# Two mixtures of experts with split fp32 weights: a slab's products ordered by weight part, and the second mixture's buffers cut six raw to four split

## The chip, the cores and the metric

The kernel runs on one core of a Trainium2 chip. The metric is the device time of one execution in microseconds: 3967.31 us is the median of three executions before the change (3966.20 to 3977.65). The trace comes from one more execution, which took 3961.94 us.

## The reference

Two transformer-like blocks follow each other on 1024 tokens of width 1024. Each ends in a mixture of experts, and only these two mixtures are touched. In the first, a router picks two of 32 experts for each token; in the second, each of 16 experts picks its 128 best tokens. What an expert does is the same in both:

```python
# first mixture, per expert e (D=1024, F=512)
hb = jax.nn.silu(xb @ w1[e]) * (xb @ w3[e]);  yb = hb @ w2[e]
# second mixture, all 16 experts (D=1024, F=2048)
gt = jnp.einsum('becd,edf->becf', xe, w_gate);  up = jnp.einsum('becd,edf->becf', xe, w_up)
ye = jnp.einsum('becf,efd->becd', jax.nn.silu(gt) * up, w_down) * vals[..., None]
x = x + jnp.zeros_like(x).at[bidx, idx].add(ye)
```

All data are fp32, and the result has to be near that of fp32.

## The kernel before

TensorE gets near fp32 by splitting. `split` (lines 41 to 44) makes of an fp32 tile a high part on ScalarE (`hi`, line 43, rounded to the matmul's own type) and the rest on VectorE (`lo`, line 44: source minus `hi`). `mm3` (lines 49 to 52) then sums three products into PSUM: high by high (L50), token-high by weight-low (L51), token-low by weight-high (L52). In the trace a matmul `h<-hi,xh` is L50, `h<-lo,xh` L51, `h<-hi,xl` L52. The tokens are the stationary operand, the weights the moving one of 512 columns, so each product loads the tokens anew (LDWEIGHTS, on the row PEld).

Weights come in slabs of 1 MB (`Unit.slab`): a raw tile of 128 partitions by 2048 numbers is asked for by a DMA on SyncE's queue, then split. Three rings of buffers pass a slab on: `raw` (pool `wraw`), and `hi` and `lo` (pool `whl`). A raw buffer is free again when `lo` is made; `hi` and `lo` are free when the slab's twelve products are done.

`Unit.up` makes silu(x W1)*(x W3) for 512 hidden columns: four slabs of four 128-row pieces each, twelve products a slab, into two PSUM tiles `h`. Then `u` is made on ScalarE and VectorE, transposed on TensorE (`pt<-ident,u`), and split into `hh` and `hl`. `Unit.down` multiplies them with two slabs into `y`, again twelve products a slab. `run_units` goes over the units; `up` of the next one stands before `down` of this one. The first mixture has 32 units of 96 tokens (one an expert; in 11 of them `down` uses raw fp32 weights, `rawn`, with no split), and beside it a filter's transform is made in small steps (`ks`, `kv`, `K_d`), called at each slab's end by `tick`. The second has 16 experts of four units each, 384 slabs in all, and nothing beside it.

A token list is looked up an expert ahead (`fetch` in `moe2`): one-hot rows `oh` on VectorE, eight small matmuls, the tile `pc` of one column, and a gather of rows `xg` by GpSimd. At an expert's end its rows `ys` are added to DRAM by a scatter on GpSimd's queue. Each engine works its instructions off in a fixed order; a scheduler has set that order when the program was built, from the order in which the code is written and the buffers that exist.

Of the kernel before, what the change touches and what calls it, by code (L numbers as in the profile page):

```python
# [11 lines left out]
F32=mybir.dt.float32; F32R=mybir.dt.float32r; I32=mybir.dt.int32; U32=mybir.dt.uint32  # L12
# [36 lines left out]
def mm3(nc, ps, sh, sl, mh, ml, start, stop):  # L49
    nc.tensor.matmul(ps, sh, mh, start=start, stop=False)  # L50
    nc.tensor.matmul(ps, sh, ml, start=False, stop=False)  # L51
    nc.tensor.matmul(ps, sl, mh, start=False, stop=stop)  # L52

def colmajor(ap, n):

    return ap.rearrange("(n p) -> p n", p=128)
# [23 lines left out]
def flat(ap):  # L80
    return ap.rearrange("p a b -> p (a b)")

def bcast_row(ap, n, off=0):

    return bass.AP(tensor=ap.tensor,offset=ap.offset+off,ap=[[0,128],[1,n]])
# [371 lines left out]
SPL=1  # L457
# [170 lines left out]
class Unit:  # L628
# [26 lines left out]
    def up(s,x,w1,w3,nat=False):  # L655

        k,nc,p,m=s.k,s.k.nc,s.p,s.m
        xh,xl=x
        hs=[]
        for w in (w1,w3):  # L660
            ps=s.ph.tile([128,512],F32,name="h")[0:m]
            for c in range(2):
                sl=s.slab(w[512*c:512*c+512],4,512)
                for j in range(4):
                    d=4*c+j
                    mm3(nc,ps,xh[:,d],xl[:,d],*sl[j],d==0,d==7)
                s.tick()
            hs.append(ps)
        u=p.tile([128,512],F32,name="u")[0:m]
        nc.scalar.activation(u,hs[0],AF.Silu)  # L670
        nc.vector.tensor_tensor(u,u,hs[1],op=ALU.mult)
        ps=s.pt.tile([128,4,m],F32,name="pt")
        for j in range(4): nc.tensor.transpose(ps[:,j],u[:,128*j:128*j+128],k.ident[0:m,0:m])
        if nat:
            ht=p.tile([128,4,m],F32R,name="hh").bitcast(F32); nc.scalar.activation(ht,ps,AF.Copy)
            return ht,None
        hh=p.tile([128,4,m],F32R,name="hh"); hl=p.tile([128,4,m],F32R,name="hl")
        split(nc,hh,hl,ps)
        return hh,hl
    def down(s,h,w2,y,first,last):  # L680
        nc=s.k.nc
        hh,hl=h
        for c in range(2):
            src=w2[256*c:256*c+256]
            if hl is None:
                raw=s.wnat.tile([128,2048],F32,name="rawn")
                raw=raw.rearrange("p (k n) -> p k n",k=2); nc.sync.dma_start(raw,src.rearrange("(k p) n -> p k n",p=128))
                for j in range(2):
                    f=2*c+j
                    for n in range(2): nc.tensor.matmul(y[0:s.m,n],hh[:,f],raw[:,j,512*n:512*n+512],start=first and f==0,stop=last and f==3)  # L690
                s.tick()
                continue
            sl=s.slab(src,2,1024)
            for j in range(2):
                f=2*c+j
                for n in range(2):
                    st,sp=first and f==0,last and f==3
                    mm3(nc,y[0:s.m,n],hh[:,f],hl[:,f],*[q[:,512*n:512*n+512] for q in sl[j]],st,sp)
            s.tick()

def run_units(U,units,ahead):
# [21 lines left out]
        z=p.tile([128,256],F32,name="z"); nc.gpsimd.memset(z,0.0)  # L723
        for d in dst: nc.gpsimd.dma_start(d[1024:1152].rearrange("p (a b) -> p a b",b=256),z[:,None,:].to_broadcast([128,4,256]))

def moe_pools(tc,es,nb,pre,nr=4):

    e=lambda *x,**y: es.enter_context(tc.tile_pool(*x,**y))
    return e(name=pre+"r",bufs=nr if nb>1 else 2),e(name=pre+"w",bufs=3*SPL if nb>1 else 2*SPL),e(name=pre,bufs=nb)

def moe1(k,a,R,fill):

# [803 lines left out]
def moe2(k,a,R,out):  # L1536
    tc,nc=k.tc,k.nc
    wg,wu,wd=a['w_gate_2'][0],a['w_up_2'][0],a['w_down_2'][0]
    acc_d,xn_d=R.acc_d,R.xn_d
    with ExitStack() as es:  # L1540
        pre=ExitStack(); pp=pre.enter_context(tc.tile_pool(name="m2p",bufs=1,side="right"))
        k.gathers=[]
        first=[pp.tile([128,2048],F32,name=f"pre{j}") for j in range(NPRE)]
        wraw,whl,p=moe_pools(tc,es,2,"m2",8)
        R.route()
        e=lambda *x,**y: es.enter_context(tc.tile_pool(*x,**y))
        ph,pt,py=e(name="m2h",bufs=4,space=PSUM),e(name="m2t",bufs=2,space=PSUM),e(name="m2y",bufs=1,space=PSUM)
# [2 lines left out]
        def unit(x,u):  # L1550
            c=slice(512*u,512*u+512)
            def fetch():
                sel=pt.tile([128,5],F32,name="pt")
                for t in range(8):
                    if t%4==0:
                        oh=p.tile([128,4,128],BF16,name="oh")
                        nc.vector.tensor_tensor(oh,R.iota[:,None,:].to_broadcast([128,4,128]),R.posT[:,t:t+4,x:x+1].to_broadcast([128,4,128]),op=ALU.is_equal)
                    nc.tensor.matmul(sel,oh[:,t%4],R.aux[:,t,x],start=t==0,stop=t==7)
                pc=p.tile([128,1],F32,name="pc"); nc.vector.tensor_copy(pc,sel[:,0:1])
                nc.vector.scalar_tensor_tensor(R.tok[:,x:x+1],sel[:,1:2],128.0,pc,op0=ALU.mult,op1=ALU.add)  # L1560
                nc.vector.tensor_reduce(R.aff[:,x:x+1],sel[:,2:5],axis=AX.X,op=ALU.add)
                return U.fetch(xn_d,R.tok[:,x:x+1])
            def down(h):
                if x==0 and u==0:
                    pre.close()
                    F['p']=e(name="fin",bufs=1,side="right"); F['w']=e(name="finw",bufs=6,side="right")
                if x==1 and u==0: F['gf']=F['p'].tile([128,1024],F32,name="gf"); nc.gpsimd.dma_start(F['gf'],bcast_row(a['g_final_2'],1024))
                if u==0: ys_[x]=py.tile([128,2,512],F32,name="y")
                U.down(h,wd[x][c],ys_[x],u==0,u==3)
            def fin():  # L1570
                y=ys_.pop(x)
                if x<15:
                    ys=p.tile([128,1024],F32,name="ys"); nc.scalar.activation(ys,flat(y),AF.Copy,scale=R.aff[:,x:x+1])
                    nc.gpsimd.indirect_dma_start(out=acc_d,out_offset=bass.IndirectOffsetOnAxis(ap=R.tok[:,x:x+1],axis=0),in_=ys,in_offset=None,compute_op=ALU.add)
                    if x==14: U.tick=lambda: next(last,None)
                else:
                    for _ in last: pass
                    z=F['rows']
                    nc.vector.scalar_tensor_tensor(z,flat(y),R.aff[:,x:x+1],z,op0=ALU.mult,op1=ALU.add)
                    r=unit_rows(k,F['p'],F['p'],z,"rd")  # L1580
                    nc.vector.scalar_tensor_tensor(z,z,r,F['gf'],op0=ALU.mult,op1=ALU.mult)
                    nc.gpsimd.indirect_dma_start(out=out,out_offset=bass.IndirectOffsetOnAxis(ap=R.tok[:,x:x+1],axis=0),in_=z,in_offset=None)
            return dict(fetch=fetch if u==0 else None,up=lambda q: U.up(q,wg[x][:,c],wu[x][:,c]),down=down,fin=fin if u==3 else None)

        F={}
# [19 lines left out]
        last=finish()  # L1605
# [52 lines left out]
```

## Time and profile before

| | us |
|---|---|
| median of three executions | 3967.31 |
| the profiled execution | 3961.94 |
| its span, first to last instruction | 3960.2 |
| first mixture, from its first weight product to the last of its `up` | 704 to 1466 |
| second mixture, from its token lists to its last products | 2776 to 3930 |

TensorE is busy 94% of the span, VectorE 78%, ScalarE 56%. Matmuls overlap each other in the trace (each is some 0.40 us long, and the next begins about 0.23 us after it), so the busy share does not tell how densely they follow; the starts do. The page's 40 slices, 99 us each, show TensorE near full in both mixtures (slices 7 to 14 and 28 to 39), and the DMA engines too. A row of waits reads: who waited, for whom, how long in all, how often, the longest.

### The profile page before, as it was taken

To read this page: it belongs to the slowest core of one execution; us is meant where nothing else is said; L and a number is where in the kernel's file an instruction comes from. 1 tells how busy PE (TensorE), PEld (TensorE's weight loads), DVE (VectorE), ACT (ScalarE), POOL (GpSimd) and SP (SyncE) were. 2 spreads that over 40 slices of the span, in tenths; PEclk is the share of its full clock that TensorE was granted. 3 is DMA by queue.
4 is the path that set the end of the run, shared out by engine and by line. 5 is a ranking of instruction groups with operands and counts; after the bars stand their busy time and mean duration, and the time that the engine had idled before them with its cause. 6 is when DMAs were issued, how large, how long until landed. Compare 5 with 4: busy or idle time off the path is not lost.

```text
span 3960.2 us, 49738 instructions
## 1 busy us (share of the span) xinstructions
PE 3733.2 (94%) x18392; PEld 2960.8 (75%) x18392; DVE 3080.9 (78%) x4728; ACT 2215.0 (56%) x2522; POOL 443.7 (11%) x469
## 2 busy tenths in 40 slices
PE   8999998899989996999999999997899999999997
PEld 6787676676766675777888887876677777777775
DVE  3655765899889886776899989644788888888887
ACT  3733653566656654884333333322577777777776
POOL 0013000323332221000000000000000100100100
PEclk9999898899999997999999999998899999999998
DMA  3235634899989974122333335635799999999997
GB/s 96 64 96 114 169 104 175 281 341 320 314 292 327 312 262 147 57 88 86 96 109 110 105 103 171 208 129 198 262 366 374 359 367 371 358 375 364 363 374 290
DMA packets 459240, 900.99 MB, mean 228 GB/s; under 512 B 41734, under 2 KB 140257, under 8 KB 458610
## 3 DMA queue, kind: packets, MB, share of 16 engines
q1 hardware_dynamic: 414578, 801.90, 58.2%
q0 software_dynamic: 42832, 92.21, 8.4%
q10 hardware_dynamic: 1584, 3.67, 0.3%
q8 instruction: 146, 2.39, 0.3%
q14 instruction: 100, 0.82, 0.1%
HBM read 795.27 MB, written 102.29 MB: 227 GB/s over the span
## 4 chain that ended last, share of the span: by engine, by line
PE 60%; DVE 9%; issue 5%; DMA 5%; ACT 4%; POOL 1%; DVEq 0%; SPq 0%; ACTq 0%; POOLq 0%
PE h L51 7%; PE h L52 7%; PE h L50 7%; PE ps L51 5%; PE ps L52 5%; PE ps L50 5%; PE y L51 4%; PE y L52 4%; PE y L50 4%; PE iv L1086 3%; DVE lo L44 2%; DMA raw<-in_expert_w 2%; PE U L1074 1%; PE ks L1023 1%; PE y L690 1%
## 5 line engine op out<-in xcount | busy, mean ns | idle before, releaser
L44 DVE TENSOR_TENSOR lo<-raw,hi 128x2048 fp32r<-128x2048 f32 x551 | 1251.7, 2288 | 146.9 <-ACT hi L43 146.2
L43 ACT ACTIVATE hi<-raw 128x2048 fp32r<-128x2048 f32 x551 | 1047.9, 1913 | 222.7 <-PE h L52 114.2
L51 PE MATMUL h<-lo,xh 128*128 128x512 f32 (+1 forms) x1536 | 617.6, 402 | 12.5 <-DVE lo L44 12.5
L50 PE MATMUL h<-hi,xh 128*128 128x512 f32 (+1 forms) x1536 | 616.7, 402 | 0.6 <-ACT xh L43 0.6
L52 PE MATMUL h<-hi,xl 128*128 128x512 f32 (+1 forms) x1536 | 610.0, 397 | 0.0
L50 PE MATMUL ps<-hTh,whi 128*128 128x512 f32 x896 | 359.1, 401 | 2.8 <-ACT ge L1252 2.8
L51 PEld LDWEIGHTS h<-lo,xh 128*128 128x128 f32 (+1 forms) x1536 | 276.9, 180 | 105.2 <-DVE lo L44 33.2
L51 PE MATMUL ps<-hTl,whi 128*128 128x512 f32 x896 | 354.9, 396 | 0.0
L52 PE MATMUL ps<-hTh,wlo 128*128 128x512 f32 x896 | 354.3, 395 | 0.0
L52 PEld LDWEIGHTS h<-hi,xl 128*128 128x128 f32 (+1 forms) x1536 | 276.5, 180 | 77.0 <-issue 0.8
L50 PEld LDWEIGHTS h<-hi,xh 128*128 128x128 f32 (+1 forms) x1536 | 277.0, 180 | 75.5 <-ACT xh L43 1.1
L51 PE MATMUL y<-lo,hh 128*128 128x512 f32 (+1 forms) x680 | 273.9, 403 | 0.5 <-DVE lo L44 0.5
L50 PE MATMUL y<-hi,hh 128*128 128x512 f32 (+1 forms) x680 | 270.1, 397 | 0.3 <-ACT hi L43 0.3
L52 PE MATMUL y<-hi,hl 128*128 128x512 f32 (+1 forms) x680 | 269.4, 396 | 0.0
L44 DVE TENSOR_TENSOR wlo<-wraw,whi 128x1024 fp32r<-128x1024 f32 x96 | 117.0, 1219 | 131.5 <-ACT whi L43 104.4
L634 POOL DMA_INDIRECT xg<-xn_d,tok x48 | 101.8, 2122 | 873.8 <-issue 795.3
L50 PEld LDWEIGHTS ps<-hTh,whi 128*128 128x128 f32 x896 | 170.7, 191 | 36.6 <-ACT ge L1252 3.3
L52 PEld LDWEIGHTS ps<-hTh,wlo 128*128 128x128 f32 x896 | 170.1, 190 | 35.8
L51 PEld LDWEIGHTS ps<-hTl,whi 128*128 128x128 f32 x896 | 170.7, 191 | 33.4 <-DVE hTl L44 0.5
L43 ACT ACTIVATE whi<-wraw 128x1024 fp32r<-128x1024 f32 x96 | 101.4, 1056 | 161.3 <-PE ps L51 147.9
L1023 PEld LDWEIGHTS ks<-leaf,F 128*128 128x128 f32 x1024 | 137.9, 199 | 53.4 <-ACT kv L1029 20.5
L1023 PE MATMUL ks<-leaf,F 128*128 128x128 f32 x1024 | 143.5, 285 | 29.8 <-ACT kv L1029 16.1
(615 smaller groups left out, 7113.4 us busy)
## 6 DMA issues: line engine op xcount, KB each, us to landing
raw<-in_expert_w SPq DMA_DIRECT2D x170, 1024.0 KB
raw<-in_w_down SPq DMA_DIRECT2D x128, 1024.0 KB
raw<-in_w_up SPq DMA_DIRECT2D x127, 1024.0 KB
raw<-in_w_gate SPq DMA_DIRECT2D x126, 1024.0 KB
wraw<-in_w_in SPq DMA_DIRECT2D x80, 512.0 KB
K<-K_d SPq DMA_DIRECT2D x256, 128.0 KB
rawn<-in_expert_w SPq DMA_DIRECT2D x22, 1024.0 KB
K_d<-kv POOLq DMA_DIRECT2D x32, 512.0 KB, 7.4
```

The lines of the kernel that those rows point to most:

```text
L43: nc.scalar.activation(hi, src, AF.Copy)
L44: (eng or nc.vector).tensor_tensor(lo, src, hi.bitcast(F32), op=ALU.subtract)
L50: nc.tensor.matmul(ps, sh, mh, start=start, stop=False)
L51: nc.tensor.matmul(ps, sh, ml, start=False, stop=False)
L52: nc.tensor.matmul(ps, sl, mh, start=False, stop=stop)
L634: s.k.gathers.append(s.k.nc.gpsimd.indirect_dma_start(out=xg,out_offset=None,in_=src_d,in_offset=bass.IndirectOffsetOnAxis(ap=idx[0:s.m],a ...
L690: for n in range(2): nc.tensor.matmul(y[0:s.m,n],hh[:,f],raw[:,j,512*n:512*n+512],start=first and f==0,stop=last and f==3)
L1023: nc.tensor.matmul(ks[:,b%4+j],F[:,b+j,q,128*s:128*s+128],o[:,j,q],start=q==0,stop=q==1)
L1074: for q in range(2): nc.tensor.matmul(U[:,j,q],F[:,2*(b+j)+q],um[:,j,q],start=True,stop=True)
L1086: for i in range(2): nc.tensor.matmul(iv[:,j,q].rearrange("p a t -> p (a t)"),Y[i][:,j,q],G[:,2*(b+j)+q,i],start=i==0,stop=i==1)
```

## The change

Three edits. First, `mmslab` takes the place of the calls of `mm3` in `up` and `down`: it goes over a slab twice, first all products with the weights' high part (token-high and token-low by turns, eight matmuls), then the four with the low part. The count of products, loads and columns is the same. Second, in the second mixture the raw ring has six buffers where it had eight, and the rings of `hi` and `lo` have four each where they had three; the sum of bytes is the same. Third, the tile `pc` is 32 numbers wide (128 bytes) and its first column is used, so each tile that is allocated behind it in its pool starts further on.

```diff
+def mmslab(nc, terms, first, last):
+    seen=set(); n=len(terms)
+    for ps,sh,sl,mh,ml,key in terms:
+        nc.tensor.matmul(ps, sh, mh, start=first and key not in seen, stop=False); seen.add(key)
+        nc.tensor.matmul(ps, sl, mh, start=False, stop=False)
+    end={t[5]:i for i,t in enumerate(terms)}
+    for i,(ps,sh,sl,mh,ml,key) in enumerate(terms):
+        nc.tensor.matmul(ps, sh, ml, start=False, stop=last and end[key]==i)
...
                 sl=s.slab(w[512*c:512*c+512],4,512)
-                for j in range(4):
-                    d=4*c+j
-                    mm3(nc,ps,xh[:,d],xl[:,d],*sl[j],d==0,d==7)
+                mmslab(nc,[(ps,xh[:,4*c+j],xl[:,4*c+j],*sl[j],0) for j in range(4)],c==0,c==1)
...
             sl=s.slab(src,2,1024)
-            for j in range(2):
-                f=2*c+j
-                for n in range(2):
-                    st,sp=first and f==0,last and f==3
-                    mm3(nc,y[0:s.m,n],hh[:,f],hl[:,f],*[q[:,512*n:512*n+512] for q in sl[j]],st,sp)
+            mmslab(nc,[(y[0:s.m,n],hh[:,2*c+j],hl[:,2*c+j],*[q[:,512*n:512*n+512] for q in sl[j]],n) for j in range(2) for n in range(2)],first and c==0,last and c==1)
...
-def moe_pools(tc,es,nb,pre,nr=4):
+def moe_pools(tc,es,nb,pre,nr=4,ns=3):
...
-    return e(name=pre+"r",bufs=nr if nb>1 else 2),e(name=pre+"w",bufs=3*SPL if nb>1 else 2*SPL),e(name=pre,bufs=nb)
+    return e(name=pre+"r",bufs=nr if nb>1 else 2),e(name=pre+"w",bufs=ns*SPL if nb>1 else 2*SPL),e(name=pre,bufs=nb)
...
-        wraw,whl,p=moe_pools(tc,es,2,"m2",8)
+        wraw,whl,p=moe_pools(tc,es,2,"m2",6,4)
...
-                pc=p.tile([128,1],F32,name="pc"); nc.vector.tensor_copy(pc,sel[:,0:1])
+                pc=p.tile([128,32],F32,name="pc")[:,0:1]; nc.vector.tensor_copy(pc,sel[:,0:1])
```

TensorE, second mixture, the first slab of an expert behind the eight lookup products `pt<-aux,oh`. Before:

```order
L1558 LDWEIGHTS oh
L1558 MATMUL pt<-aux,oh 128x5
L50 MATMUL h<-hi,xh 128x512
L51 MATMUL h<-lo,xh 128x512
L52 MATMUL h<-hi,xl 128x512
L50 MATMUL h<-hi,xh 128x512
L51 MATMUL h<-lo,xh 128x512
L52 MATMUL h<-hi,xl 128x512
```

After (L58 and L59 are the first loop of `mmslab`, L62 the second):

```order
L1562 LDWEIGHTS oh
L1562 MATMUL pt<-aux,oh 128x5
L58 MATMUL h<-hi,xh 128x512
L59 MATMUL h<-hi,xl 128x512
L58 MATMUL h<-hi,xh 128x512
L59 MATMUL h<-hi,xl 128x512
L58 MATMUL h<-hi,xh 128x512
L59 MATMUL h<-hi,xl 128x512
L58 MATMUL h<-hi,xh 128x512
L59 MATMUL h<-hi,xl 128x512
L62 MATMUL h<-lo,xh 128x512 x4
L58 MATMUL h<-hi,xh 128x512
```

The slab's `lo` was read by the second product and is now read by the ninth; its `hi` was read until the twelfth and is now read until the eighth.

TensorE, second mixture, where the transposes of `u` stand among the products of the first `down` slab. Before:

```order
L52 MATMUL h<-hi,xl 128x512
L50 MATMUL y<-hi,hh 128x512
L51 MATMUL y<-lo,hh 128x512
L52 MATMUL y<-hi,hl 128x512
L50 MATMUL y<-hi,hh 128x512
L673 MATMUL pt<-ident,u 128x128 x4
L51 MATMUL y<-lo,hh 128x512
```

After:

```order
L62 MATMUL h<-lo,xh 128x512 x4
L58 MATMUL y<-hi,hh 128x512
L59 MATMUL y<-hi,hl 128x512
...
L62 MATMUL y<-lo,hh 128x512 x3
L681 MATMUL pt<-ident,u 128x128 x4
L62 MATMUL y<-lo,hh 128x512
```

The four transposes came behind four of the slab's products and now come behind eleven.

GpSimd's queue, second mixture, gathers of token rows (`xg`) and scatters of an expert's rows (`ys`), with buffer numbers. Before:

```order
L634 DMA xg_25274<-xn2_d_69,tok2_22054 128x1024
L634 DMA xg_25801<-xn2_d_69,tok2_22054 128x1024
L1574 DMA x3_d_68<-ys_25781,tok2_22054 1024x1024
L634 DMA xg_26328<-xn2_d_69,tok2_22054 128x1024
L1574 DMA x3_d_68<-ys_26308,tok2_22054 1024x1024
```

After:

```order
L644 DMA xg_25274<-xn2_d_69,tok2_22054 128x1024
L1578 DMA x3_d_68<-ys_25781,tok2_22054 1024x1024
L644 DMA xg_25801<-xn2_d_69,tok2_22054 128x1024
L1578 DMA x3_d_68<-ys_26308,tok2_22054 1024x1024
L644 DMA xg_26328<-xn2_d_69,tok2_22054 128x1024
```

A gather that stood ahead of the scatter of the same moment now stands behind it.

## Rows read from the trace of the kernel before

**Rows 1.** The page: busy time, share of the span and instructions of each engine.

```profile
PE 3733.2 (94%) x18392; PEld 2960.8 (75%) x18392; DVE 3080.9 (78%) x4728; ACT 2215.0 (56%) x2522; POOL 443.7 (11%) x469
```

**Rows 2.** Busy time by stage: length, engines' busy us, clock, DMA share, GB/s.

```profile
core 0: us, PE busy (x) PEld busy (x) DVE busy (x) ACT busy (x) POOL busy (x), PEclk, DMA share, GB/s
...
704.00:1466.00 762.00, 728.72 (x3805) 525.37 (x3806) 677.14 (x1001) 478.24 (x468) 229.89 (x185) 0.98 0.94 313
...
2776.00:3930.00 1154.00, 1133.56 (x5103) 897.10 (x5104) 985.50 (x624) 820.81 (x560) 83.57 (x33) 0.99 0.99 358
```

**Rows 3.** Waits in the second mixture, 2776 to 3930.

```profile
ACT hi L43 <- PE h L52: 79.4, 133, 4.3
...
PEld h L51 <- DVE lo L44: 23.5, 43, 1.1
...
PE h L51 <- DVE lo L44: 7.5, 12, 0.7
```

**Rows 4.** Timeline, second mixture, an expert's second slab waits for its `lo`.

```profile
3303.96 0.68 DVE L1557 TENSOR_TENSOR oh<-iota,posT 128x512 bf16<-128x512 bf16 x1
...
3305.29 4.48 DVE L44 TENSOR_TENSOR lo<-raw,hi 128x2048 fp32r<-128x2048 f32 x2
...
3306.57 0.40 PE L50 MATMUL h<-hi,xh 128*128 128x512 f32 x1
...
3307.63 0.50 PE L51 MATMUL h<-lo,xh 128*128 128x512 f32 x1 [0.66 <-DVE lo L44]
3307.97 0.40 PE L52 MATMUL h<-hi,xl 128*128 128x512 f32 x1
...
3315.67 0.40 PE L52 MATMUL h<-hi,xl 128*128 128x512 f32 x1
```

**Rows 5.** Timeline, second mixture, a wait that holds only the load.

```profile
3250.34 0.39 PE L50 MATMUL h<-hi,xh 128*128 128x512 f32 x1
...
3250.65 0.19 PEld L51 LDWEIGHTS h<-lo,xh 128*128 128x128 f32 x1 [0.36 <-DVE lo L44]
3250.65 0.50 PE L51 MATMUL h<-lo,xh 128*128 128x512 f32 x1
3250.99 0.40 PE L52 MATMUL h<-hi,xl 128*128 128x512 f32 x1
```

**Rows 6.** Groups by line and shape, 2900 to 3850: busy us, mean ns, idle before.

```profile
L44 DVE TENSOR_TENSOR lo<-raw,hi 128x2048 fp32r<-128x2048 f32 x320 | 724.5, 2288 | 86.2 <-ACT hi L43 86.0
L43 ACT ACTIVATE hi<-raw 128x2048 fp32r<-128x2048 f32 x320 | 607.2, 1914 | 72.1 <-PE h L52 59.2 <-PE y L52 12.9
```

**Rows 7.** DMA in 2900 to 3850: GB/s in 40 slices of 23.75 us, landing times.

```profile
GB/s 393 375 334 396 351 351 396 352 338 395 369 344 395 358 341 395 367 346 395 362 342 395 357 343 394 364 346 394 365 343 394 356 340 393 371 340 393 363 353 393
...
x_d<-ys,tok POOLq DMA_INDIRECT x13, 11.2
xg<-xn_d,tok POOLq DMA_INDIRECT x13, 9.6
```

**Rows 8.** Waits in the first mixture, 704 to 1466.

```profile
ACT hi L43 <- DMA raw<-in_expert_w: 54.2, 29, 5.8
...
ACT hi L43 <- PE h L52: 34.8, 36, 3.0
...
ACT kv L1029 <- DMA K_d<-kv: 15.8, 4, 9.5
...
PE ks L1023 <- ACT kv L1029: 12.7, 4, 8.4
...
PEld h L51 <- DVE lo L44: 9.7, 14, 1.4
...
PE h L51 <- DVE lo L44: 5.0, 9, 1.1
```

**Rows 9.** The chain that ended last, first mixture, shares of the stretch by line.

```profile
by line: DMA raw<-in_expert_w 10.8%; issue 10.8%; DVE lo L44 9.4%; PE h L50 7.2%; PE h L51 7.2%; PE h L52 7.2%; PE ks L1023 6.1%; PE y L690 4.6%; PE y L51 2.9%; PE y L52 2.9%; PE y L50 2.8%; DMA K_d<-kv 2.7%; ACT hi L43 2.3%; PE pt L641 1.7
```

## The prediction

> **What bounds the kernel now.** I read the page first: TensorE is busy 94% of the span, and it has as many weight loads as matmuls [rows 1]. That share hides small gaps, because matmuls overlap in the trace, so it is no proof that TensorE is the bound. Next I cut the span into stages. The two mixtures, the only places that the change touches, take 762 us and 1154 us; TensorE, VectorE and the DMA engines are all near full in both, and the clock is near its full level throughout, 0.98 and 0.99 of 2.4 GHz [rows 2]. So the question in each is which of the three is waited for last.
>
> In the second mixture the waits answer it. ScalarE, which takes a raw slab first, waits for TensorE to free a `hi` buffer, 79.4 us in the stage [rows 3]; in 950 us of it all of its 72.1 us of waiting before `hi` is put down to products, none to a DMA [rows 6]. So the slabs are there, and TensorE is what the others wait for. It is dense: 33 products from 3307.97 to 3315.67 us, 0.233 us apart [rows 4]. Where is it not dense? Its loads of tokens for a product with `lo` wait for VectorE 43 times, 23.5 us in all; 12 of these waits are long enough that the matmul itself shows idle time, 7.5 us [rows 3]. The reader should see the cause in the timeline: VectorE had just made one-hot rows for the next lookup, so `lo` began at 3305.29 and took 2.29 us; TensorE's product with `hi` started at 3306.57, and the one with `lo` only at 3307.63 [rows 4, 6].
>
> In the first mixture the picture is mixed. ScalarE waits for raw slabs from DRAM 29 times, 54.2 us, and for TensorE 36 times, 34.8 us; loads wait for `lo` 14 times, of which 9 reach the matmul [rows 8]. The chain of work that ended last goes through the raw DMA for 10.8% of the stage and through `lo` for 9.4%, 82 and 72 us [rows 9]. No single engine is the bound there.
>
> **The change, part by part.** *Products by weight part, second mixture.* `lo` was read by a slab's second product and is read by its ninth now, seven products or 7 x 0.233 = 1.63 us later. The longest wait for it is 1.1 us [rows 3], so all 43 should go. What one costs is read from starts, less the normal 0.233. A long one: 3306.57 to 3307.63 is 1.06 us, 0.83 too much, and the product behind it comes after 0.34 us, 0.11 too much; together 0.94 us [rows 4]. A short one: 0.31 us, 0.08 too much, and then 0.34 us, 0.11 too much; together 0.19 us [rows 5]. The sum is 12 x 0.94 + 31 x 0.19 = 11.3 + 5.9 = 17.2 us. Bounds: below, the 7.5 us of idle time that the matmuls show; above, all 23.5 us for which loads waited and 43 x 0.11 for the products behind, 28 us. I take 17.2, as it is counted from starts.
>
> *The same, first mixture.* At the same prices 9 x 0.94 + 5 x 0.19 = 9.5 us. Here the bounds are wide. Below, nothing: if the raw DMA sets the pace, a gap that is closed opens again elsewhere. Above, all of TensorE's idle time, 762 - 728.7 = 33 us: `hi` is read until the eighth product instead of the twelfth, so ScalarE may start 4 x 0.233 = 0.93 us earlier in each of its 36 waits for a buffer, and through `lo` the raw buffer is asked for earlier. I take 9.5, since both kinds of wait are there in like number [rows 8].
>
> *What the order costs.* The old order used the same tokens for two products in a row, the new one changes them at each. A load is issued for every matmul anyway [rows 1], it takes 0.19 us and lies under a product of 0.233 [rows 5]: nothing. `lo` is free 0.23 us later than before, but VectorE's next `lo` waits for ScalarE's `hi` first, 1.9 us of work: nothing. The transposes of `u` come seven products, 1.6 us, later; what they feed is read by the next unit's `down`, behind four or more slabs of 12 x 0.233 = 2.8 us: nothing. A gather now stands behind a scatter on GpSimd's queue; behind it wait the gather's landing, 9.6 us, and tokens that are used two units of some 17.8 us later (six slabs each, 950 us over 320 slabs being 2.97 us a slab) [rows 6, 7]: nothing.
>
> *Four split slabs, six raw.* The fourth pair of `hi` and `lo` lets the split run one slab, 2.97 us, further ahead of TensorE; with the waits for `lo` gone already it has nothing left to give, except a cushion. The raw ring loses more than it gives: a raw buffer came round every 8 x 2.97 = 23.8 us and now every 6 x 2.97 = 17.8 us. Of that the split takes 1.91 + 2.29 = 4.2 us [rows 6], so a slab has 13.6 us from its request to its landing, where it had 19.6. A slab's own landing time stands in no row. The nearest rows are the scatter and the gather that share the DMA engines with it, 11.2 and 9.6 us [rows 7]. Both lie under 13.6, so I cost the six buffers at nothing; above, a slab late by a whole place in the ring, 2.97 us an expert, 16 x 2.97 = 48 us.
>
> *The wider `pc`.* The copy into it still writes one column. The tiles behind it move; nothing in the trace makes a product or a split depend on where its tile begins, and it is too small to crowd anything out. I take nothing, from below and above.
>
> *The sum.* 17.2 + 9.5 = 26.7 us. The profiled execution took 3961.94 us (its span 3960.2 and 1.7 us around it), which gives 3935.2; it was 5.4 us under the median of the runs. Against the median the forecast is 3967.3 - 26.7 = 3940.6 us. A measurement tells about 0.3%, 12 us, from no change.
>
> **The rivals.** *Memory is the bound in both mixtures.* Then TensorE's gaps are only where its spare time shows, and closing them moves the wait to the raw slab: 3967 us. For it: the DMA share is 0.94 and 0.99 [rows 2], and in the first mixture ScalarE does wait for slabs [rows 8]. Against it, in the second: no wait for a slab before `hi` [rows 6], and in 14 of 40 pieces the DMA moves 393 to 396 GB/s against a mean of 358 for the stage [rows 2, 7]; a stream at its limit would not have a tenth in hand. The same answer comes out if the first mixture's order turns against it: ScalarE's `kv` waits for a DMA up to 9.5 us and TensorE then up to 8.4 us [rows 8], and three more such meetings eat 25 us. The Trainium skill speaks for this rival: "SBUF — State Buffer", section "A bandwidth-pool intuition that's wrong (but worth ruling out)", puts memory to one core at about 358 GB/s. The stage's mean is just that, so by the page alone the gain would be nothing, but the pieces at 393 to 396 in the trace do not agree with it as a limit.
>
> *Six raw buffers are too few.* Each expert's scatter and gather bring the DMA down to some 340 GB/s for a piece [rows 7]. The rival decides when a slab lands more than 13.6 us after its request and the fourth split slab's 2.97 us do not cover it. Then TensorE waits 2.97 us an expert: 48 - 26.7 = 21 us more, 3988 us. For it: 11.2 us for the scatter is within 2.4 us of the point. Against it: with eight buffers not one wait of this kind is seen, and the ring of four behind it is new cover.
>
> *Both upper bounds hold.* 28 + 33 = 61 us less, 3906 us. For it: the chain's 72 us on `lo` in the first mixture [rows 9]. Against it: that chain's 82 us on the raw DMA stay.
>
> **How the numbers follow.** I give the forecast 0.58, memory (or the first mixture's order) giving it all back 0.22, too few raw buffers 0.12, both upper bounds 0.08. The first mixture's 0 to 33 and the second's 7.5 to 28 us, not both at one end, make the likeliest case's own range 3918 to 3955. The range that is to hold 8 times in 10 takes in memory's 3967 with its spread and most of the larger gain, and leaves out the late slabs: 3912 to 3970. Faster by over 0.3% has the forecast and the larger gain, 0.66; within 0.3%, 0.22; slower, 0.12.
>
> **What the profile after would show.** Right: in the second mixture no wait for `lo` by a load or a product, the stage some 17 us shorter with products still 0.233 us apart, and still no wait for a raw slab before `hi`; in the first the stage about 10 us shorter, with fewer waits for `lo`. Wrong: products further apart (the loads were not hidden); ScalarE waiting for `in_w_gate`, `in_w_up` or `in_w_down` (six buffers are too few); the first mixture as long as it was with its waits put down to raw slabs, or to `kv` and `K_d` (memory, or the order). What would upset the forecast most is a first mixture that goes its own way: its bounds are wider than the whole gain of the second.

## The result and the profile after

The changed kernel takes 3993.45 us, median of six executions (3988.13 to 3999.83), against 3968.39 for the kernel before on the same chip: a ratio of 1.0055, 95% interval 1.004 to 1.0071. It is slower by half a per cent where a gain of 0.7% was forecast. The profiled execution took 3994.54 us.

The page and the windows by stage, beside [rows 1] and [rows 2]:

```profile
PE 3740.5 (94%) x18392; PEld 2954.3 (74%) x18392; DVE 3071.8 (77%) x4728; ACT 2198.7 (55%) x2522; POOL 424.5 (11%) x469
```

```profile
core 0: us, PE busy (x) PEld busy (x) DVE busy (x) ACT busy (x) POOL busy (x), PEclk, DMA share, GB/s
707.00:1478.00 771.00, 731.48 (x3807) 526.45 (x3808) 678.38 (x1002) 478.94 (x469) 221.72 (x185) 0.98 0.94 309
2793.00:3963.00 1170.00, 1137.46 (x5097) 888.90 (x5097) 971.87 (x621) 800.53 (x557) 72.49 (x33) 0.99 0.99 355
```

The page shows next to nothing. The windows show that the second mixture got longer with the same clock and the same DMA share. To compare many kernels I measure a mixture from the start of its first weight product to the start of its last. The first mixture went from 779.5 to 787.8 us, the second from 1142.7 (2791.3 to 3934.0, a little past the window of [rows 2]) to 1158.5. The rest of the profiled difference lies ahead of the first mixture (3 us) and between the two (5 us), in instructions that the change leaves alone.

Waits in the second mixture of the kernel after, beside [rows 3]:

```profile
DVE lo L44 <- ACT hi L43: 186.6, 152, 4.7
ACT hh L43 <- PE pt L681: 179.2, 63, 4.2
ACT u L678 <- PE h L62: 130.6, 58, 2.8
PEld h L62 <- DVE lo L44: 66.3, 111, 0.7
...
PE h L62 <- DVE lo L44: 18.8, 81, 0.3
...
ACT hi L43 <- PE h L59: 18.0, 22, 3.5
```

And two rows that the kernel before has for ScalarE in 2776 to 3930:

```profile
ACT hh L43 <- PE pt L673: 135.5, 62, 2.3
...
ACT u L670 <- PE h L52: 65.7, 63, 1.8
```

The waits for `lo` were to vanish. They went from 43 to 111 for loads and from 12 to 81 for products, although `lo` is now read seven products later. ScalarE hardly waits for a buffer any more (79.4 us before, 18.0 now); it waits at `u` (twice as long) and at `hh`. The groups by shape show the same and clear the raw ring, beside [rows 6], 2920 to 3870:

```profile
L44 DVE TENSOR_TENSOR lo<-raw,hi 128x2048 fp32r<-128x2048 f32 x312 | 703.2, 2288 | 154.3 <-ACT hi L43 154.1
L43 ACT ACTIVATE hi<-raw 128x2048 fp32r<-128x2048 f32 x312 | 576.5, 1906 | 1.4 <-DMA raw<-in_w_up 0.8 <-DVE lo L44 0.6
```

Of all its splits in 950 us ScalarE waited for a raw slab once, 0.8 us. One unit in the timeline of the kernel after:

```profile
3230.44 5.51 ACT L43 ACTIVATE hi<-raw 128x2048 fp32r<-128x2048 f32 x3
3238.69 0.60 ACT L678 ACTIVATE u<-h 128x512 f32<-128x512 f32 x1 [2.74 <-PE h L62]
3239.18 5.51 ACT L43 ACTIVATE hi<-raw 128x2048 fp32r<-128x2048 f32 x3
...
3241.12 4.49 DVE L44 TENSOR_TENSOR lo<-raw,hi 128x2048 fp32r<-128x2048 f32 x2 [2.05 <-ACT hi L43]
3241.14 0.19 PEld L58 LDWEIGHTS h<-hi,xh 128*128 128x128 f32 x1 [0.20 <-ACT hi L43]
...
3243.47 0.30 PEld L62 LDWEIGHTS h<-lo,xh 128*128 128x128 f32 x2 [0.64 <-DVE lo L44]
3243.47 0.50 PE L62 MATMUL h<-lo,xh 128*128 128x512 f32 x1 [0.22 <-DVE lo L44]
```

Read it from the top. ScalarE is done with three splits at 3235.95 and then stands at `u` until TensorE has finished the unit's first two slabs, 2.74 us. The split of the fourth slab stands behind `u`. It ends at 3241.1, TensorE wants it at that moment, and VectorE, which had stood idle 2.05 us, makes `lo` so late that even the ninth product waits. In the program's order `u` stood behind the `hi` of its unit's fourth slab in all 64 units before; it stands behind that of the third in 55 of 64 after.

The chain that ended last in the second mixture tells it in shares. Before, 2776 to 3930, its first six entries were products, 90% together, and `lo` had 2.3%:

```profile
by line: PE h L51 20.5%; PE h L52 19.7%; PE h L50 19.5%; PE y L51 10.3%; PE y L52 10.2%; PE y L50 10.2%; issue 3.7%; PE pt L673 2.7%; DVE lo L44 2.3%; PE pt L641 1.3%; DVE oh L1557 0.6%; DMA xg<-xn_d,tok 0.4%; PE pt L1558 0.3%; ACT hi L43 0
```

After, 2793 to 3963:

```profile
by line: DVE lo L44 18.2%; PE h L62 15.1%; ACT hi L43 13.1%; PE y L59 8.3%; PE y L58 8.3%; issue 8.2%; PE y L62 8.0%; PE h L58 6.9%; PE h L59 6.7%; DMA raw<-in_w_down 4.4%; PE pt L681 2.2%; PE pt L651 0.8%; DMA xg<-xn_d,tok 0.7%; ACT xh L43
```

The 4.4% for `raw<-in_w_down` are five slabs of `down` that landed, 8.4 to 11.2 us after their request, just as ScalarE came to them: six raw buffers left nothing in hand there. It is not what the change loses, as the experiments show.

First mixture, 707 to 1478, beside [rows 8]:

```profile
ACT hi L43 <- DMA raw<-in_expert_w: 87.0, 41, 5.9
...
ACT hi L43 <- PE h L59: 49.0, 47, 2.5
...
PE ks L1027 <- ACT kv L1033: 19.1, 6, 6.2
...
PEld h L62 <- DVE lo L44: 0.3, 1, 0.3
```

Here the waits for `lo` did vanish, 14 to 1 for loads, and came back as waits for raw slabs (54.2 to 87.0 us) and for the filter's `kv` (12.7 to 19.1).

### The profile page after: what moved, and what is told of

Read it like the earlier page. It is cut to its first block, busy times and chain, and to the rows that moved or that the text cites. A ratio compares the mean times of both kernels' runs of the same rounds, so it can differ in the third digit from the quotient of the medians.

```text
span 3992.8 us, 49759 instructions
## 1 busy us (share of the span) xinstructions
PE 3740.5 (94%) x18392; PEld 2954.3 (74%) x18392; DVE 3071.8 (77%) x4728; ACT 2198.7 (55%) x2522; POOL 424.5 (11%) x469
## 4 chain that ended last, share of the span: by engine, by line
PE 44%; DVE 12%; ACT 8%; DMA 6%; issue 6%; POOL 1%; ACTq 0%; DVEq 0%; POOLq 0%; SPq 0%
DVE lo L44 6%; PE h L62 5%; PE ps L51 5%; PE ps L52 5%; PE ps L50 5%; ACT hi L43 4%; PE h L58 3%; PE h L59 3%; PE y L59 3%; PE y L58 3%; PE y L62 3%; PE iv L1090 3%; DMA raw<-in_expert_w 2%; PE U L1078 1%; DMA raw<-in_w_down 1%
## 5 line engine op out<-in xcount | busy, mean ns | idle before, releaser
L43 ACT ACTIVATE hi<-raw 128x2048 fp32r<-128x2048 f32 x551 | 1031.6, 1910 | 206.8 <-DMA raw<-in_expert_w 89.8
L58 PE MATMUL h<-hi,xh 128*128 128x512 f32 (+1 forms) x1536 | 617.4, 402 | 1.0 <-ACT xh L43 0.6
L59 PE MATMUL h<-hi,xl 128*128 128x512 f32 (+1 forms) x1536 | 605.8, 394 | 0.0
L62 PE MATMUL h<-lo,xh 128*128 128x512 f32 (+1 forms) x1536 | 433.4, 402 | 19.3 <-DVE lo L44 18.8
L62 PEld LDWEIGHTS h<-lo,xh 128*128 128x128 f32 (+1 forms) x1536 | 265.1, 179 | 132.7 <-DVE lo L44 66.5
L58 PEld LDWEIGHTS h<-hi,xh 128*128 128x128 f32 (+1 forms) x1536 | 276.6, 180 | 86.3 <-ACT hi L43 19.7
L59 PEld LDWEIGHTS h<-hi,xl 128*128 128x128 f32 (+1 forms) x1536 | 277.0, 180 | 66.1 <-issue 0.4
L58 PE MATMUL y<-hi,hh 128*128 128x512 f32 (+1 forms) x680 | 268.8, 395 | 0.0
L59 PE MATMUL y<-hi,hl 128*128 128x512 f32 (+1 forms) x680 | 268.7, 395 | 0.0
L62 PE MATMUL y<-lo,hh 128*128 128x512 f32 (+1 forms) x680 | 199.7, 400 | 0.0
L50 PE MATMUL ps<-xTh,whi 128*128 128x512 f32 x400 | 159.0, 398 | 0.1
```

What stands on the lines that cost most here:

```text
L43: nc.scalar.activation(hi, src, AF.Copy)
L58: nc.tensor.matmul(ps, sh, mh, start=first and key not in seen, stop=False); seen.add(key)
L59: nc.tensor.matmul(ps, sl, mh, start=False, stop=False)
L62: nc.tensor.matmul(ps, sh, ml, start=False, stop=last and end[key]==i)
```

## The experiments

Each was timed beside the kernel before, on the same chip. Two stage numbers carry the reading: the second mixture's length (first to last weight product), and the spacing of its 4608 weight products, which is the mean start-to-start distance of neighbours below 250 ns (anything longer holds a wait or another instruction). Three theories stood at the start: A, the transposes of `u`, moved from behind 4 products of `down` to behind 11, hold ScalarE at `hh`; B, the order that the new rings give ScalarE; C, slabs that land late with six raw buffers.

**Order or rings.** `order_83` is the change without its rings and `pc`; `order_m2_83` has the new order in the second mixture alone; `rings_64` only the rings:

```diff
-        wraw,whl,p=moe_pools(tc,es,2,"m2",8)
+        wraw,whl,p=moe_pools(tc,es,2,"m2",6,4)
```

```diff
-                for j in range(4):
...
+                if s.m==128:
+                    mmslab(nc,[(ps,xh[:,4*c+j],xl[:,4*c+j],*sl[j],0) for j in range(4)],c==0,c==1)
+                else:
```

(the second diff is that of `order_m2_83` in `up`; `s.m` is 128 tokens in the second mixture and 96 in the first, and `down` has the same condition).

> The new order alone, in both mixtures; the rings stay at eight raw and three split slabs, pc stays narrow. Theory A (the order itself: the transposes of u stand behind 11 products of down where they stood behind 4, so ScalarE stands longer at hh, its next hi and VectorE's lo come late, and TensorE waits at a slab's ninth product): all of the loss is here. The second mixture, 1143 us before and 1159 in the change from its first product to its last, takes about 1159, the first about 8 more than before, the whole about 3993; ScalarE's waits at hh come to about 150 us in 2920 to 3870. Theory B (the rings: with four split slabs ScalarE's queue is ordered otherwise, with hi ahead of u and hh): the second mixture takes at most 1143, the whole about 3976 from the first mixture alone. Theory C (six raw slabs are too few, so slabs land late): as B.

> The new order in the second mixture alone, rings eight and three, pc narrow. Theory A (the order there moves the transposes of u behind 11 products): the second mixture takes about 1159 us, the whole about 3984. Theories B and C (the rings): at most 1143 and 3968.

> The rings alone: six raw and four split slabs in the second mixture, the old order of products, pc narrow. Theory A: no loss, 3960 to 3970; the fourth split slab may take some of the 43 waits for lo away. Theory B: the second mixture takes about 1159, the whole about 3984, with ScalarE's waits at u and hh as long as in the change. Theory C: the same 3984, but with ScalarE waiting for raw slabs before hi.

| | ratio to before | second mixture |
|---|---|---|
| before | 1 | 1142.7 |
| after | 1.0055 [1.004, 1.0071] | 1158.5 |
| order_83 | 1.0067 [1.0049, 1.0086] | 1164.6 |
| order_m2_83 | 1.0058 [1.0041, 1.0074] | 1165.4 |
| rings_64 | 1.002 [1.0007, 1.0032] | 1143.1 |

The order alone costs 22 us in the second mixture, the rings nothing there. That falls against B and C. In the chain of `order_83`, with eight raw buffers, no raw slab stands, and its second mixture is no shorter than that of the change. The order alone also moves `u`: it stands behind its unit's third `hi` in 54 of 64 units of `order_83` and in none of `rings_64`. The whole of `rings_64` is some 8 us longer than before all the same. Its second mixture doesn't show them, and its first mixture (799.1 us) runs the same instructions as before, in an execution 11 us above the kernel's median; where the 8 us lie stays open.

**Transposes back at 4 products.** `trans4_64` is the change, with `down`'s first slab held behind the transposes from its fifth product on; `trans4_83` the same with rings eight and three:

```diff
+            pin=s.k.tc.issue_after(s.tr.ins) if c==0 and s.m==128 else None
...
+        if pin and i==2: pin.__enter__()
```

> The whole change, and beside it one thing: in the second mixture the products of down's first slab from the fifth on are held behind the four transposes of u, so that these stand behind 4 products again, as before the change. Theory A: ScalarE's waits at hh fall from 159 us to about 120 or less in 2920 to 3870, the waits for lo go, and the second mixture takes 1126 to 1143, the whole 3960 to 3977 (the first mixture still carries its 8 us). If the transposes now wait for u, TensorE shows it at pt and part of this is lost. Theories B and C: nothing moves, about 3993.

> The new order in both mixtures with the transposes of u held at 4 products of down in the second, rings eight and three, pc wide. Theory A: as with rings six and four, the second mixture 1126 to 1143 us, the whole 3960 to 3977. If the fourth split slab is what lets the order pay, this one is slower than that with six and four by some us, and its waits for lo stay. Theory C (raw slabs too few at six): this one is the faster of the two.

1.0057 [1.0041, 1.0074] and 1.0058 [1.0043, 1.0074]; the second mixture 1158.3 and 1160.2 us. Nothing was won, so A falls as it stood. Waits of `trans4_64`, 2850 to 3900:

```profile
ACT u L680 <- PE h L63: 156.2, 55, 4.0
...
PEld pt L683 <- DVE u L681: 46.3, 54, 1.1
PE pt L683 <- DVE u L681: 25.6, 37, 0.7
```

The wait has moved: TensorE now stands at the transposes because `u` comes late, and ScalarE still stands at `u`. `u` itself was in the wrong place, and that became theory D.

**The new order in `up` alone.** `order_up2_64` keeps the old order in `down` and the first mixture: the condition `s.m==128` in `up` as above, `mm3` in `down`, rings six and four, `pc` narrow.

> The new order only in the slabs of up in the second mixture, four of six slabs of each unit; down and the first mixture keep the old order; rings six and four; pc narrow. In the program the transposes of u then stand behind 4 products. Theory A: no loss in the first mixture, and in the second the waits for lo in up go, so 1130 to 1143 us there and 3950 to 3968 in all. Theories B and C: the second mixture takes about 1159, the whole about 3984.

1.0117 [1.0098, 1.0137], the second mixture 1184.6 us: the worst so far, and it was to be among the best. The transposes stand behind 4 products here, but `u` stands behind the third slab in 42 of 64 units. Waits, 2850 to 3900:

```profile
ACT u L683 <- PE h L62: 168.1, 54, 4.3
...
PEld y L51 <- DVE lo L44: 45.9, 38, 1.2
PE y L51 <- DVE lo L44: 29.4, 38, 0.8
```

The lateness reaches `down`, whose old order wants `lo` at the second product and pays more for it.

**`u` put back, and put forward.** `ulead2_64` is the change with `u` held behind the fourth slab's `hi`; `ulead2_trans4_64` holds the transposes too; `before_ulead1` is the kernel before with the fourth slab's `hi` held behind `u`:

```diff
-        nc.scalar.activation(u,hs[0],AF.Silu)
+        with s.k.tc.issue_after(s.hi.ins) if m==128 else nullcontext(): nc.scalar.activation(u,hs[0],AF.Silu)
```

> The whole change, and beside it one thing: in the second mixture ScalarE's u is held behind the hi of its unit's fourth up slab. In the change u stands behind the third in most units, so ScalarE stands at u, for TensorE's first two slabs, with the fourth slab not yet split; before the change it stands behind the fourth. Theory D (the place of u is the cause): ScalarE's waits at u fall from 123 us in 2850 to 3900 to about 60, the waits for lo at the ninth product go, and the second mixture takes 1121 us or less (the wide pc alone gave 1121 with the old order), the whole 3935 to 3965. Theory A (the transposes' place is the cause, still behind 11 products here): 1150 to 1159 us and about 3990. If it takes both, something between, 1130 to 1145.

> The whole change with both things held: u behind the hi of the fourth up slab, and the transposes of u behind 4 products of down. With the transposes held alone TensorE waited at pt for u, 26 us with 46 of its loads, since u came late. Theory D: with u not stuck ahead of a split, that wait goes too, and the second mixture takes 1100 to 1121 us, the whole 3925 to 3960. Rival: u now comes still later (it has one more hi, 1.9 us, ahead of it), so TensorE waits at pt longer than the 26 us and the second mixture stays at 1150 or more.

> The kernel before, with the suspected cause put in alone: in the second mixture the hi of each unit's fourth up slab is held behind u. Order of products, rings and pc are as before; the transposes move with u, behind 12 products in most units. Theory D: the second mixture takes 20 to 40 us longer than its 1143, with ScalarE's waits at u about doubled from 60 us and TensorE waiting for lo at a slab's second product; the whole about 3990 to 4005. Rival (it is the order of a slab's products by itself): at most 1147 us and 3960 to 3975.

The second mixture, with the change's order, rings and `pc`:

| | transposes behind 11 | behind 4 |
|---|---|---|
| `u` mostly behind the third slab's `hi` | 1158.5 (after) | 1158.3 (`trans4_64`) |
| `u` behind the fourth slab's `hi` | 1125.0 (`ulead2_64`) | 1099.7 (`ulead2_trans4_64`) |

The wholes of the lower row are 0.9974 [0.996, 0.9989] and 0.991 [0.9889, 0.993] of before. `u`'s place is worth 33 to 59 us; the transposes' place is worth nothing while `u` is late and 25 once it is not. `ulead2_64` shows the second cost by itself: ScalarE's waits at `u` have fallen (123.3 us in the change, 27.1 here), and those at `hh` have grown (166.3 and 231.8), 2850 to 3900:

```profile
ACT hh L43 <- PE pt L682: 231.8, 59, 4.2
...
ACT u L679 <- PE h L63: 27.1, 28, 2.4
```

With both held, the list of that stretch holds no wait of a weight product for `lo`, and ScalarE's waits for slabs stay small. ScalarE still waits long at `hh` and `u`; what counts is what stands behind them:

```profile
ACT hh L43 <- PE pt L684: 157.4, 61, 2.7
...
ACT u L681 <- PE h L64: 88.8, 58, 4.0
...
ACT hi L43 <- DMA raw<-in_w_up: 5.2, 9, 0.8
```

The margin shows it slab by slab: the end of a slab's `lo` to the start of the first product that reads it, median over 56 units (the fifth to the sixtieth), us (0.05 is the least there is, a product that waited):

| | first slab | third | fourth | sixth |
|---|---|---|---|---|
| before | 0.26 | 1.35 | 1.39 | 0.45 |
| after | 0.21 | 1.22 | 0.05 | 1.14 |
| `trans4_64` | 1.79 | 2.40 | 0.06 | 2.02 |
| `ulead2_64` | 0.21 | 1.22 | 1.74 | 1.93 |
| `ulead2_trans4_64` | 1.79 | 2.49 | 3.01 | 2.01 |

The fourth slab answers to `u`: its `lo` was waited for in 51 of the 56 units of the change, in none before and in none of `ulead2_64`. The first answers to the transposes: 25 of 56 waited before, in the change and in `ulead2_64`, none where they are held. `before_ulead1` confirms the direction and misses in size: 1.0257 [1.0232, 1.0283], and 1247.1 us where 1163 to 1183 were expected. The transposes moved with `u` in most units (38 of 64), and TensorE here waits for `hi` itself; how the 64 us beyond the forecast's 1183 divide between the two is not shown:

```profile
ACT u L664 <- PE h L52: 186.5, 54, 4.1
...
PE y L50 <- ACT hi L43: 69.1, 55, 1.3
```

**The wide `pc` by itself.**

```diff
-                pc=p.tile([128,1],F32,name="pc"); nc.vector.tensor_copy(pc,sel[:,0:1])
+                pc=p.tile([128,32],F32,name="pc")[:,0:1]; nc.vector.tensor_copy(pc,sel[:,0:1])
```

> The wider lookup tile alone. Every theory here: no change, 3960 to 3972. If tiles that begin elsewhere cost something, the products or splits of the second mixture take longer one by one, and the whole comes out above 3980.

0.9957 [0.994, 0.9974]: 17 us faster, 21 in the second mixture, from an edit that I had costed at nothing. Its timeline shows where; 26 weight products with no wait among them, the first and the last:

```profile
3239.67 0.39 PE L51 MATMUL h<-lo,xh 128*128 128x512 f32 x1
...
3245.33 0.39 PE L52 MATMUL h<-hi,xl 128*128 128x512 f32 x1
```

5.66 / 25 is 0.226 us a product, where it was 0.233 [rows 4]. The granted clock is not the reason: from 2850 to 3900 it is 1.00 in the kernel before, in `pc_wide` and in the five kernels that follow. `pc` lies ahead of the tokens, so a wider `pc` moves `xh`, `xl`, `hh` and `hl` by a whole number of 64 bytes. Five more kernels vary that: `pc_24`, `pc_16` and `pc_72` set other widths; `shift_all` leaves 192 bytes free ahead of the split slabs, so that slabs and tokens move together; `shift_hilo` adds a 48-column `pc`, so that the slabs alone move.

```diff
+    if pre=="m2": e(name="pad",bufs=1).tile([128,48],F32,name="pad")
```

> The kernel before with pc 24 columns (96 bytes) wide, so that the tiles behind its two buffers, the tokens xh and xl and the products' hh and hl among them, begin 64 bytes behind a multiple of 128, as with the narrow pc; with 32 columns they begin at a multiple. Theory (where the tiles begin is what made the wide pc faster): products 233 ns apart, the second mixture 1143 us, the whole 3957 to 3978. Rival (the width of pc itself, or distance between its two buffers, does it): products 227 ns apart, 1121 us and about 3949.

> The kernel before with pc 16 columns wide (64 bytes): xh, xl, hh and hl then begin at a multiple of 512 bytes; with the narrow pc they begin 448 behind one, and products are 233 ns apart; with 24 columns 64 behind (229), with 32 columns 128 behind (227). Theory E (a 128-column row of 512 bytes that begins at 448 of 512 costs more; at a small remainder less): 226 to 229 ns, the second mixture 1118 to 1128 us, the whole 3940 to 3955. Rival (it is the width, or the number of bytes that the tiles have moved, not the remainder): 16 columns move them by only 64 bytes, so something between 233 and 229 ns, 1128 to 1143 us.

> The kernel before with pc 72 columns wide (288 bytes): the tiles move by 512 bytes, so xh, xl, hh and hl begin 448 behind a multiple of 512 again, as with the narrow pc. Theory E: 233 ns and 1143 us again, 3957 to 3978 in all. Rival (width or distance): 227 to 229 ns, 1121 to 1128 us, about 3950.

> The kernel before with 192 unused bytes ahead of the split slabs, so that these (hi, lo) and the tokens (xh, xl, hh, hl) all begin 192 bytes later: the tokens 128 behind a multiple of 512 as with the 32-column pc, the split slabs 64 behind one where they were 384 behind; the distance between the two is as before. Theory F (where the tokens begin decides): products 227 ns apart, the second mixture 1121 us, the whole about 3950. Rival G (the distance between slabs and tokens decides): 233 ns, 1143 us, about 3966.

> The same 192 bytes, with pc 48 columns wide so that the tokens begin 448 behind a multiple of 512 as before; the split slabs alone begin elsewhere, 64 behind one. Theory F: 233 ns, 1143 us, about 3966. Rival G, or that the slabs' own place decides: another spacing, 226 to 232 ns.

Where tokens and split slabs begin, modulo 512 bytes, and what follows:

| | slabs | tokens | distance | spacing, ns | second mixture | ratio to before |
|---|---|---|---|---|---|---|
| before | 384 | 448 | 64 | 233.3 | 1142.7 | 1 |
| `pc_72` | 384 | 448 | 64 | 233.3 | 1141.5 | 0.9986 [0.9973, 0.9999] |
| `shift_all` | 64 | 128 | 64 | 233.3 | 1142.5 | 1.0 [0.9989, 1.0011] |
| `pc_16` | 384 | 0 | 128 | 232.5 | 1139.9 | 0.9991 [0.9978, 1.0004] |
| `shift_hilo` | 64 | 448 | 384 | 232.6 | 1139.7 | 0.999 [0.998, 1.0001] |
| `pc_24` | 384 | 64 | 192 | 229.1 | 1127.3 | 0.9953 [0.9937, 0.9969] |
| `pc_wide` | 384 | 128 | 256 | 227.6 | 1121.3 | 0.9957 [0.994, 0.9974] |

What I expected of `pc_24`, that the remainder by 128 decides and 24 columns leave 233 ns, was a miss. My theory E (a row of 512 bytes that begins late in its line costs more) was half right: `pc_72` falls back to 233 ns as it says, but `pc_16`, which begins at 0, should have been fast and is not. Theory F (the tokens' own place) fails at `shift_all`: tokens at 128, and 233 ns. What all seven agree with is G, the distance between slabs and tokens: slow at 64, a little faster at 128, faster at 192, fastest at 256. The distance of 384 goes with 128. It is 128 short of 512 and also 128 past 256, so these seven do not tell whether the pattern repeats after 512 bytes or after 256; a distance of 0 or 320 would, and none was run. The order of the products has no part in it: with the narrow `pc` the new order has 233.3 ns too (`order_83`), with the wide one 227.3 to 229.1.

**The first mixture.** `order_m1_83` has the new order there alone (the condition turned to `s.m<128`); `held_m1old_64` is `ulead2_trans4_64` with the old order there; `ulead2_trans4_83` is `ulead2_trans4_64` with rings eight and three.

> The new order in the first mixture alone; the second mixture's order, rings and pc are as before. If the first mixture's order costs by itself what the two traces show (703 to 711 us from its first product to the last add being 8 us longer), the whole is about 3976 and the first mixture some 8 us longer, with waits for lo nearly gone and longer waits for raw slabs, kv and the sums of the filter. Rival: the 8 us were chance in where transfers fell; then the first mixture is 0 to 10 us shorter and the whole 3958 to 3968.

> The change with u held behind the fourth slab's hi and the transposes at 4 products, as in the run before, but with the old order of products in the first mixture. If the new order costs the first mixture some 8 us, this is 5 to 10 us faster than with it, 3920 to 3928, and the first mixture takes 775 to 785 us from its first product to its last. If the spread there (775 to 799 us for the same instructions) hides everything, the two stand within 5 us of each other. If the new order helps in the first mixture after all, this one is the slower.

> The change with both held, but with eight raw and three split slabs. If the fourth split slab is only a cushion that nothing needs, the second mixture takes 1100 us as with six and four (1099.7) and the whole is within 5 us of 3931. If it is what lets the new order pay, this one takes 1110 us or more there, with ScalarE waiting before hi for TensorE.

`order_m1_83`: 1.0014 [1.0002, 1.0025], the first mixture 791.4 us, the second 1141.4 as before, and again the raw slabs:

```profile
ACT hi L43 <- DMA raw<-in_expert_w: 89.2, 44, 7.1
ACT hi L43 <- PE h L59: 50.2, 45, 2.5
```

The held pair tells less: 0.9903 [0.9883, 0.9923] with the old order, 0.991 with the new, and 783.9 against 793.4 us for the stage. Over all profiles the first mixture took 775 to 799 us in the twelve kernels with the old order there (mean 784.9) and 785 to 793 in the eight with the new one (mean 790.4). Each group runs one and the same sequence of instructions there, so the spread among the twelve is not the kernels'. It goes with how far the profiled execution lay from the median of its own kernel (799.1 us in `rings_64`, 11 above its median; 775.2 in `pc_wide`, 14 below; correlation 0.90 over the twelve). With that taken out by a straight line, the new order costs the first mixture 6.0 us, standard error 1.4: it gains nothing there and loses a little. The rings: 1104.5 us in the second mixture with eight and three, 1099.7 with six and four, the wholes 0.9917 [0.9898, 0.9937] and 0.991. The new rings are worth 5 us at most, once both are held.

The fastest kernels are thus `ulead2_trans4_64` and `held_m1old_64`, at 3931.23 and 3930.59 us: some 36 us under the kernel before and 62 under the change. Nearly half of the 36 is the wide `pc`, which gave 17 alone; the rest is the order, the rings and the two holds.

## Why the prediction was wrong

**The step that failed** is "What the order costs". Its terms are all put at nothing, and by `order_83` the order made the second mixture 22 us longer where it was to make it 17.2 shorter. At the transposes it says: "what they feed is read by the next unit's `down`, behind four or more slabs of 12 x 0.233 = 2.8 us: nothing." It asked who reads the result, and not who stands behind the reader. `hh` is an instruction in ScalarE's queue with the next slabs' `hi` behind it; a late transpose delays those (25 us once nothing else does). In the same sum I followed the moved transposes on TensorE and gathers on GpSimd, and did not look at ScalarE's order, in which the same change had put `u` ahead of the fourth slab's split. That was the larger loss, 33 to 59 us. The term for the loads held: products are 233.3 ns apart in either order. The Trainium skill says in "PSUM — Partial Sum Buffer", section "Engine vs sequencer instructions", that the queues of ScalarE, VectorE and GpSimd are strictly first in, first out; the trace agrees, with a split that stood 2.74 us behind `u`. Why the scheduler, given the new order of products, chose that place for `u` no run shows.

**The 43 waits for `lo`, 17.2 us.** Right in mechanism and size, once the rest is held. Distances of 250 ns or more between weight products cost 26.2 us above the mean spacing in the kernel before and 9.2 in `ulead2_trans4_64`: 17.0 us, though with another `pc` and other rings. With both alike, `pc_wide` and `ulead2_trans4_83`, the stage goes from 1121.3 to 1104.5 us: 16.8 us. That the two come so near to 17.2 is in part luck, since the price came from one long and one short wait. In the change itself such distances cost 64.9, since the wait for `lo` had grown past the seven products of cover.

**The wider `pc`, nothing.** Wrong by 21 us: "nothing in the trace makes a product or a split depend on where its tile begins". The trace of before had one address pattern only and could not show it; the honest bounds were a few nanoseconds on each of 4608 products, to either side. (233.3 - 227.6) x 4608 is 26 us; the stage gained 21. In the change most of it is buried: with the order at fault, the second mixture takes 1165 us with the narrow `pc` and 1158 with the wide one, because TensorE waits for the splits (the rings differ too; `trans4_83`, with the wide `pc` and the old rings, has 1160).

**The first mixture, 9.5 us.** Wrong: some 6 us lost. The waits for `lo` closed as said, and longer waits for raw slabs and for `kv` came in their place, as the rival of memory, or of the first mixture's order, had it there.

**Six raw and four split slabs.** Right in the second mixture: ScalarE waits 0.8 us for a slab in the change and some 6 with both held, the five landings in the chain, 8.4 to 11.2 us, lie under the 13.6 that were reckoned, and the cushion is worth little. The gather behind the scatter: behind the stage's first weight product TensorE waits for no gather.

**Memory as the bound in the second mixture.** It shared 0.22 with the first mixture's order and is refuted there, by the windows of `ulead2_trans4_64`:

```profile
2803.00:3903.00 1100.00, 1100.00 (x5106) 900.43 (x5104) 970.52 (x613) 807.58 (x565) 83.34 (x31) 1.00 1.02 376
```

The same slabs came at 376 GB/s over the whole stage, so the 358 of the kernel before were the pace that it asked for. The Trainium skill puts memory to one core at about 358 GB/s ("SBUF — State Buffer", section "A bandwidth-pool intuition that's wrong (but worth ruling out)"); as a limit that does not hold in this trace, and the measurement decides.

The sum for the second mixture, then: -17.2 became +22 (the order with its two misplaced instructions), and 0 became -6 (what the wide `pc` and the rings could still give, 1164.6 to 1158.5): 15.8 us slower. The remaining 9 us of the medians lie in or around the first mixture, some 6 of them in it.

## What to carry to other kernels

Where a scheduler sets the order, an edit on one engine is costed only when the order of every engine that feeds it has been read again; an instruction that waits for a result in an in-order queue costs what stands behind it, not only what reads it. Hold such an instruction behind the work that it must not block, and an order that lost 22 us in its stage can win 17 there. A tile that only moves other tiles is an edit too: try it alone, and read the spacing of products from starts.

## What the hardware showed unasked

In these kernels the spacing of 128x128 by 128x512 fp32r products goes with where the stationary tokens begin relative to the moving slab, by remainders modulo 512 bytes: 233.3 ns at a distance of 64, 232.5 at 128, 229.1 at 192, 227.6 at 256. Loads took 188 ns with the narrow and the wide `pc` alike, 2900 to 3850:

```profile
L51 PEld LDWEIGHTS h<-lo,xh 128*128 128x128 f32 x851 | 159.8, 188 | 57.2 <-DVE lo L44 21.4
L51 PEld LDWEIGHTS h<-lo,xh 128*128 128x128 f32 x865 | 162.3, 188 | 57.0 <-DVE lo L44 25.0
```

The Trainium skill, in "SBUF — State Buffer", section "A bandwidth-pool intuition that's wrong (but worth ruling out)", gives TensorE a second, independent read port for its weight loads; the measured 2.5% between the slowest and the fastest distance may mean that the two reads are not wholly independent, or that something else in the pair depends on where its tiles lie. Which, no run here shows.
